# Two tables of a convolution stage: twelve taps of one half tile to the array's 32x32 parts, and another place for three merges

## The chip, the core and the metric

The kernel runs on one NeuronCore of a Trainium2 chip. Its engines work side by side, each through its own queue in order: TensorE (PE) multiplies matrices, VectorE (DVE) and ScalarE (ACT) do elementwise work, GpSimd (POOL) and SyncE (SP) mostly issue transfers. The metric is the device time of one execution in microseconds. Three runs of the kernel before took 1189.69, 1190.68 and 1196.95 us; the median is 1190.68 us.

## What is computed

A two-layer decoder trunk over 512 positions and 1024 channels. Layer 0 mixes with a state-space group and an attention; layer 1 mixes with the convolution module below. Each layer ends with two normalised residual steps. The change lies in the convolution of layer 1 and in what follows at once.

```python
def conformer_conv(x, w_pw1, b_pw1, w_dw, b_dw, ln_g, ln_b, w_pw2, b_pw2):
    h = x @ w_pw1 + b_pw1
    val, gate = jnp.split(h, 2, axis=-1)
    h = val * jax.nn.sigmoid(gate)
    h = lax.conv_general_dilated(            # causal, depthwise, 31 taps
        h, w_dw[:, None, :], window_strides=(1,), padding=[(CONV_SIZE - 1, 0)], ...)  + b_dw
    h = jax.nn.silu(layer_norm(h, ln_g, ln_b))
    return h @ w_pw2 + b_pw2
...
x = layer_norm(DEEPNORM_ALPHA * x + mix, ln1_g[layer], ln1_b[layer])
```

## The kernel before

Channels lie on partitions. The 1024 channels are eight tiles of 128, numbered 0 to 7, and a tile holds all 512 positions, or, where work is split, two halves of 256 positions (`HALVES`). A product of float32 matrices is made of three products of parts (`gemm`, line 225): each weight and each activation is kept as a high and a low part, and high x high, low x high and high x low are summed in PSUM. So one projection tile is 24 matmuls.

The convolution stage is written as a list of tokens, `CONV_ORDER`, that `step` works off one by one. After each token `in_order` chains every PE, DVE and ACT instruction of it behind the one before on its engine, so the list is the order of these three queues. A token is a letter, a tile, and, where it has a third character, a half (`40` is tile 4, first half; `41` its second half):

- `g`: the projections of a tile, value (`pv`) and gate (`pg`), 24 matmuls each; then a sigmoid on ACT (`csg`) and a product on DVE that writes the tile `hp`. `u` is the value projection alone, so that a later `g` of the same half has only the gate left.
- `v`: one part of the taps of a tile on DVE (`taps_dve`): each tap is one SCALAR_TENSOR_TENSOR into `cy` or `cz` in turn. A full tile's taps come in 5 parts, a half tile's in 4 (`PARTS`). The first part also makes ACT open `cy` and `cz` with the two last taps. `f` is the same in one go, for tiles with few or no taps on DVE. At the end `cy` and `cz` are summed and the tile is added to the running sum `sc` of its half, from which the mean comes.
- `p`: the first `PE_TAPS[half][tile]` taps on PE (`taps_32`, line 1126): for each tap four matmuls on 32x32 parts of the array, one for each group of 32 channels, with diagonal weights `D` that DVE makes (`d`, line 1134). The taps land in four PSUM tiles `cw`, since tap t uses column group t mod 4.
- `c`: ACT copies the four `cw` to SBUF (`cq`, line 1140). `m`: four PE matmuls sum them into `cn` (`merge`, line 1146). ACT or DVE then puts `cn` into `cy`.
- `M`, `Q`, `n`: the layer norm over channels of one half. `M` makes the mean on PE (`mpc`), subtracts it on DVE, squares on ACT (`sqc`) and adds on DVE. `Q` makes the variance on PE (`vpc`) and its inverse root: a table load and one activation (`rc`) on ACT, three steps on DVE (`tc`, `rc`). Each `n` takes two tiles: DVE multiplies `cy` by `rc`, ACT applies silu (another table load ahead of the first), and the result is split into `csh` (ACT) and `csl` (DVE).
- `t`: one output tile of the next projection `tld` (24 matmuls of 256 positions on all eight `csh`/`csl`), added to X on DVE. From the first `t` on the list runs inside `tail_norm_lead`, which makes the remaining `t` of both halves and the next norm.
- `x`: scales X on ACT.

PSUM has six tiles `nps` for projections, `cw` and `tld`, and two `stp` for `cn`, `mpc` and `vpc`. `hid` tiles (16) hold `hp`, `cz`, `D` and `cq`.

```python
PE_TAPS = ((0, 0, 24, 0, 0, 24, 31, 31), (0, 0, 0, 0, 0, 0, 31, 31))
PARTS = (5, 4)
```

Only tile 4 and tile 7 have tokens by halves. So the second row of `PE_TAPS` matters for these two: before, tile 4's second half has all its 29 remaining taps on DVE, 7, 7, 7 and 8 in the four `v41`.

## Time and profile before

| | before |
|---|---|
| three runs | 1189.69, 1190.68, 1196.95 us |
| the profiled execution's own time | 1188.93 us |
| its span in the trace | 1187.2 us |
| PE busy | 98 % |
| DVE, ACT busy | 64 %, 43 % |
| TensorE's mean granted clock | 0.993 |
| convolution stage, from tile 2's projections to the first `tld` | about 651 to 762 us in the span |

A row of the timeline gives start, duration, engine, line, operation, output and inputs, shapes and, in brackets, how long the engine had been idle and what ended it. Matmuls overlap: what one costs in a row of its kind is the distance of two starts, not its duration. A float32 matmul stands as two records in the trace (`cw`, `cn`, `mpc`, `vpc`), one of the split parts as one.

### The profile page before, as it was taken

The page shows a single profiled execution, that of the slowest core. Times are in us where ns is not written, and L with a number is a line of the kernel's source. Part 1 is how long each engine was busy: PE and PEld are TensorE (multiplying, and loading weights), DVE is VectorE, ACT ScalarE, POOL GpSimd, SP SyncE. Part 2 cuts the span into 40 slices and gives each one's busy share as a digit, 9 for nine tenths or more (in the row PEclk, how much of TensorE's full clock was granted, in tenths as well). Part 3 has the DMA queues.
Part 4 walks back from the last instruction along what each step waited for, and adds up shares of the span by engine and source line. Part 5 has one row for each costly group of instructions (what it writes and reads, how often), then busy time and mean ns, then how long its engine had stood idle before and what let it go on. Part 6 is the DMA issues. An engine that isn't in the chain of part 4 may idle for free.

```text
span 1187.2 us, 17722 instructions
## 1 busy us (share of the span) xinstructions
PE 1158.6 (98%) x7148; PEld 969.0 (82%) x7148; DVE 754.7 (64%) x1342; ACT 506.7 (43%) x798; POOL 67.0 (6%) x125
## 2 busy tenths in 40 slices
PE   9989999999999999999999999899999999999997
PEld 7777767799888888888999676699988888888885
DVE  7999876498545545546466899876833443434446
ACT  7857869336335335325223312552741421413220
POOL 1022211000000000000021120001000000000000
PEclk9999999999999999999999999899999999999999
DMA  9611321332788788779274451206241232323211
GB/s 213 168 50 51 93 67 57 105 107 80 244 286 293 238 287 297 247 274 306 91 263 161 145 181 35 73 3 211 89 143 61 99 124 71 107 86 110 73 51 71
DMA packets 132546, 169.58 MB, mean 143 GB/s; under 512 B 13874, under 2 KB 105778, under 8 KB 132464
## 3 DMA queue, kind: packets, MB, share of 16 engines
q1 hardware_dynamic: 123664, 136.96, 35.6%
q0 software_dynamic: 8640, 31.46, 7.9%
q8 instruction: 56, 0.92, 0.3%
q14 instruction: 26, 0.21, 0.1%
q10 hardware_dynamic: 160, 0.03, 0.0%
HBM read 132.12 MB, written 35.65 MB: 141 GB/s over the span
## 4 chain that ended last, share of the span: by engine, by line
PE 82%; DVE 8%; ACT 4%; DMA 3%; issue 1%; SPq 1%; POOL 0%; DVEq 0%; ACTq 0%; POOLq 0%
PE f L225 23%; PE g L1311 12%; PE acf L225 11%; PE tld L225 4%; PE tlb L225 4%; PE fl L225 3%; PE pv L225 3%; PE h L1295 3%; PE pg L225 3%; PE cw L1126 2%; PE tla L225 2%; PE acmo L225 2%; PE pl L225 2%; DVE wlo L102 1%; DMA raw<-in_ffn_w_dram 1%
## 5 line engine op out<-in xcount | busy, mean ns | idle before, releaser
L102 DVE TENSOR_TENSOR wlo<-raw,whi 128x1024 fp32r<-128x1024 f32 x176 | 213.3, 1223 | 199.7 <-ACT whi L101 197.5
L101 ACT CAST whi<-raw 128x1024 fp32r<-128x1024 f32 x176 | 182.1, 1049 | 322.0 <-PE g L1311 106.8
L1311 PE MATMUL g<-whi,hh 128*128 128x512 f32 x208 | 81.6, 392 | 0.0
L1311 PE MATMUL g<-whi,hl 128*128 128x512 f32 x208 | 81.6, 392 | 0.0
L1311 PE MATMUL g<-wlo,hh 128*128 128x512 f32 x208 | 81.5, 392 | 0.0
L225 PE MATMUL f<-xah,whi 128*128 128x512 f32 x208 | 81.0, 390 | 0.0
L225 PE MATMUL f<-xdh,whi 128*128 128x512 f32 x208 | 81.0, 389 | 0.0
L225 PE MATMUL f<-xdh,wlo 128*128 128x512 f32 x208 | 80.9, 389 | 0.0
L225 PE MATMUL f<-xal,whi 128*128 128x512 f32 x208 | 80.9, 389 | 0.0
L225 PE MATMUL f<-xdl,whi 128*128 128x512 f32 x208 | 80.9, 389 | 0.0
L225 PE MATMUL f<-xah,wlo 128*128 128x512 f32 x208 | 80.9, 389 | 0.0
L225 PE MATMUL acf<-hl,whi 128*128 128x512 f32 x192 | 75.6, 394 | 0.0
L225 PE MATMUL acf<-hh,whi 128*128 128x512 f32 x192 | 75.6, 394 | 0.0
L225 PE MATMUL acf<-hh,wlo 128*128 128x512 f32 x192 | 75.4, 393 | 0.0
L215 ACT CAST hh<-fr 128x512 fp32r<-128x512 f32 x64 | 39.7, 620 | 59.0 <-DVE fr L353 59.0
L216 DVE TENSOR_TENSOR hl<-fr,hh 128x512 fp32r<-128x512 f32 x64 | 44.1, 690 | 31.1 <-ACT hh L215 31.1
L353 DVE TENSOR_TENSOR fr<-fr 128x512 f32<-128x512 f32 x64 | 43.7, 685 | 14.4 <-ACT fr L154 14.4
L357 DVE SCALAR_TENSOR_TENSOR cy<-hp,wdw,cy 128x512 f32<-128x512 f32 (+1 forms) x81 | 52.2, 646 | 0.0
L357 DVE SCALAR_TENSOR_TENSOR cz<-hp,wdw,cz 128x512 f32<-128x512 f32 (+1 forms) x74 | 47.6, 643 | 0.0
L88 POOL DMA_DIRECT2D whi<-kepth x30 | 16.1, 536 | 556.8 <-PE tlb L225 386.3
L1311 PEld LDWEIGHTS g<-wlo,hh 128*128 128x128 f32 x208 | 39.1, 188 | 8.7
L1311 PEld LDWEIGHTS g<-whi,hl 128*128 128x128 f32 x208 | 39.0, 188 | 8.8
(631 smaller groups left out, 2890.4 us busy)
## 6 DMA issues: line engine op xcount, KB each, us to landing
raw<-in_ffn_w_dram SPq DMA_DIRECT2D x48, 1024.0 KB, 5.6
raw<-in_ffn_w_dram SPq DMA_DIRECT2D x32, 512.0 KB, 3.7
kepth<-whi SPq DMA_DIRECT2D x30, 512.0 KB, 3.6
keptl<-wlo SPq DMA_DIRECT2D x30, 512.0 KB, 9.3
whi<-kepth POOLq DMA_DIRECT2D x30, 512.0 KB, 3.6
wlo<-keptl POOLq DMA_DIRECT2D x30, 512.0 KB, 4.9
raw<-in_conv_w_pw_dram SPq DMA_DIRECT2D x12, 1024.0 KB, 7.1
raw<-in_mix_w_in_dram SPq DMA_DIRECT2D x16, 512.0 KB, 4.1
```

Source lines behind the costliest of these rows:

```text
L88: nc.gpsimd.dma_start(x, d)
L101: i0 = nc.scalar.copy(hi, raw).ins
L102: i1 = nc.vector.tensor_sub(lo, raw, hi.bitcast(F32)).ins
L215: i0 = S.copy(hi, src).ins
L216: i1 = V.tensor_sub(lo, src, hi.bitcast(F32)).ins
L225: ins = PE.matmul(ps[:, c0:c1], u[:, k, ksl], v[:, c0:c1], start=start and k == 0 and i == 0, stop=stop and k == n - 1 and i == 2).ins
L353: V.tensor_tensor(o, x, y, op=op)
L357: V.scalar_tensor_tensor(o, x, s, y, op0=op0, op1=op1)
L1126: PE.matmul(cps[j, c0][g][C, :], Ds[j][t // 16][R, t % 16, :], hps[j][R, t + c0 : t + c1], start=t < 4, stop=t >= n - 4, tile_position=(R. ...
L1295: PE.matmul(ps, u, v, start=k == 0 and i == 0, stop=k == nk - 1 and i == 2)
L1311: PE.matmul(pss[b], u, v[:, kk, :], start=k + kk == 0 and i == 0, stop=k + kk == nb - 1 and i == 2)
```

## The change

Two tables are rewritten, and nothing else.

```diff
-PE_TAPS = ((0, 0, 24, 0, 0, 24, 31, 31), (0, 0, 0, 0, 0, 0, 31, 31))
+PE_TAPS = ((0, 0, 24, 0, 0, 24, 31, 31), (0, 0, 0, 0, 12, 0, 31, 31))
-CONV_ORDER = "d2 g0 g1 v0 v0 g2 v0 v0 g3 p2 v1 c2 x0 v1 v1 v1 m2 f2 v0 g4 v1 v3 v3 g5 d5 v3 g6 p5 d7 d6 v3 c5 v3 m5 f5 g70 p6 v40 v40 c6 v40 m6 f6 v40 p70 c70 u71 m70 f70 M0 g71 v41 Q0 v41 p71 n0 n0 n0 n0 v41 t c71 v41 t m71 f71 t t M1 t Q1 n1 n1 n1 n1".split()
+CONV_ORDER = "d2 g0 g1 v0 v0 g2 v1 v0 v0 g3 p2 v1 c2 x0 v1 v1 v0 g4 m2 f2 v1 v3 v3 g5 d5 v3 g6 p5 d7 d6 v3 c5 v3 g70 m5 f5 p6 v40 d4 v40 c6 v40 u71 m6 f6 v40 p70 c70 v41 m70 f70 p41 M0 g71 v41 Q0 c41 p71 m41 n0 n0 n0 n0 v41 t c71 v41 t m71 f71 t M1 Q1 n1 n1 n1 n1".split()
```

Tile 4's second half now has 12 taps on PE (`p41`: 48 matmuls, with `d4`, `c41` and `m41`) and 17 on DVE, 4, 4, 4 and 5 in the four `v41`. The merges `m2`, `m5`, `m6` stand behind `g4`, `g70` and `u71`. One part `v1` stands ahead of `g3`. The first `v41` stands ahead of `m70`; none stands between `Q0` and `n0` any more, where `c41`, `p71` and `m41` stand. Of the `t`, three instead of four stand ahead of `M1`, and none between `M1` and `Q1`; the others follow.

On PE, the first merge (`cw2`, `cn2` are tile 2's taps and their merge, `pv4`, `pg4` tile 4's projections, `pv5` tile 5's). Before:

```order
L1126 MATMUL cw203_6330<-hp2_6177,D21_6148 32x512
L1146 MATMUL cn20_6470<-cq200_6436,mask_3281 32x512
...
L1146 MATMUL cn20_6470<-cq203_6439,mask_3281 32x512
L225 MATMUL pv40_6506<-xbh0_5585,whi130_6186 128x512
```

In the change:

```order
L1126 MATMUL cw203_6339<-hp2_6177,D21_6148 32x512
L225 MATMUL pv40_6486<-xbh0_5585,whi130_6186 128x512
...
L225 MATMUL pg40_6487<-xbh7_5599,wlo131_6191 128x512
L1146 MATMUL cn20_6540<-cq200_6442,mask_3281 32x512
...
L1146 MATMUL cn20_6540<-cq203_6445,mask_3281 32x512
L225 MATMUL pv50_6593<-xbh0_5585,whi132_6194 128x512
```

The 48 matmuls of tile 4's projection now stand between the taps and their merge. `m5` and `m6` moved in the same way, behind 48 and 24 matmuls.

On ACT, from the gate of tile 7's second half (`csg7256`) to the first silu. Before:

```order
L160 ACTIVATE csg7256_7332<-pg7256_7245,PV_86 128x256
L154 ACTIVATE cy4_7056<-hp4_6497,PV_86,wdw_3280 128x256
L154 ACTIVATE cz4_7057<-hp4_6497,wdw_3280 128x256
L156 ACT_TABLE_LOAD
L160 ACTIVATE rc0_7349<-vpc0_7344,cb_83 128x256
L156 ACT_TABLE_LOAD
L160 ACTIVATE cy0_6162<-cy0_6162,PV_86 128x256
```

In the change:

```order
L160 ACTIVATE csg7256_7392<-pg7256_7092,PV_86 128x256
L156 ACT_TABLE_LOAD
L160 ACTIVATE rc0_7404<-vpc0_7399,cb_83 128x256
L1140 COPY cq42560_7427<-cw42560_7286 128x256
L1140 COPY cq42561_7428<-cw42561_7287 128x256
...
L1140 COPY cq42563_7430<-cw42563_7289 128x256
L156 ACT_TABLE_LOAD
L160 ACTIVATE cy0_6162<-cy0_6162,PV_86 128x256
```

The two openings of tile 4's second half went ahead of the mean, and the four copies of its taps came in between `rc` and the second table load.

On DVE, from the inverse root to the first normalised tile. Before:

```order
L357 SCALAR_TENSOR_TENSOR tc0_7350<-vpc0_7344,rc0_7349 128x256
L353 TENSOR_TENSOR tc0_7350<-tc0_7350,rc0_7349 128x256
L357 SCALAR_TENSOR_TENSOR rc0_7349<-tc0_7350,rc0_7349 128x256
L357 SCALAR_TENSOR_TENSOR cz4_7057<-hp4_6497,wdw_3280,cz4_7057 128x256
...
L353 TENSOR_TENSOR cy0_6162<-cy0_6162,rc0_7349 128x256
L353 TENSOR_TENSOR cy1_6427<-cy1_6427,rc0_7349 128x256
```

In the change:

```order
L357 SCALAR_TENSOR_TENSOR tc0_7405<-vpc0_7399,rc0_7404 128x256
L353 TENSOR_TENSOR tc0_7405<-tc0_7405,rc0_7404 128x256
L357 SCALAR_TENSOR_TENSOR rc0_7404<-tc0_7405,rc0_7404 128x256
L353 TENSOR_TENSOR cy0_6162<-cy0_6162,rc0_7404 128x256
L353 TENSOR_TENSOR cy1_6252<-cy1_6252,rc0_7404 128x256
```

The seven taps that stood between `rc` and the first normalised tile are gone from there.

## Rows read from the trace of the kernel before

**Rows 1.** The page, section 1 (busy time, share of the span, instructions of each engine) and the line of section 2 with the granted TensorE clock in 40 slices of the span.

```profile
PE 1158.6 (98%) x7148; PEld 969.0 (82%) x7148; DVE 754.7 (64%) x1342; ACT 506.7 (43%) x798; POOL 67.0 (6%) x125
PEclk9999999999999999999999999899999999999999
```

**Rows 2.** Busy time of each engine in stretches of the span: from and to, length, PE, PE weight loads, DVE, ACT, POOL with their instructions in brackets, granted clock, DMA share, GB/s.

```profile
720.00:740.00 20.00, 19.38 (x419) 13.01 (x430) 19.76 (x42) 4.62 (x9) 0.00 (x0) 1.00 0.01 3
740.00:760.00 20.00, 17.17 (x452) 13.15 (x448) 16.79 (x45) 8.95 (x19) 2.11 (x4) 1.00 0.32 109
775.00:800.00 25.00, 25.00 (x196) 24.39 (x197) 17.80 (x50) 15.17 (x29) 0.12 (x1) 1.00 0.00 1
800.00:1150.00 350.00, 349.92 (x1760) 297.56 (x1759) 167.07 (x240) 122.21 (x174) 6.21 (x12) 1.00 0.32 104
```

**Rows 3.** Timeline of PE: the merges of tiles 2, 5 and 6, and that of tile 7's first half (128x256).

```profile
675.27 2.51 PE L1146 MATMUL cn<-cq,mask 128*32 128x512 f32 x8 [0.69 <-ACT cq L1140]
...
717.78 2.51 PE L1146 MATMUL cn<-cq,mask 128*32 128x512 f32 x8 [0.62 <-ACT cq L1140]
...
735.41 2.51 PE L1146 MATMUL cn<-cq,mask 128*32 128x512 f32 x8 [0.62 <-ACT cq L1140]
...
746.38 0.64 PE L1146 MATMUL cn<-cq,mask 128*32 128x256 f32 x8
```

**Rows 4.** Timeline of PE, 737 to 762 us without the projections: taps of tile 7's first half, mean, variance, taps of its second half, first matmul of `tld`.

```profile
737.86 4.60 PE L1126 MATMUL cw<-hp,D 32*32 32x256 f32 x218
...
742.66 0.72 PE L1126 MATMUL cw<-hp,D 32*32 32x256 f32 x30 [0.21 <-issue]
...
748.24 0.67 PE L915 MATMUL mpc<-sc,ones 128*128 128x256 f32 x2 [1.22 <-DVE sc L353]
...
752.08 1.99 PE L915 MATMUL vpc<-sqc,ones 128*128 128x256 f32 x8 [0.30 <-DVE sqc L353]
754.00 3.39 PE L1126 MATMUL cw<-hp,D 32*32 32x256 f32 x160
758.48 2.06 PE L1126 MATMUL cw<-hp,D 32*32 32x256 f32 x88 [1.09 <-issue]
761.87 0.39 PE L225 MATMUL tld<-csh,whi 128*128 128x256 f32 x1 [1.33 <-ACT csh L215]
```

**Rows 5.** Timeline of PE: the first matmul of the second `tld` tile, the merge behind it, the first matmul of the third tile, and the mean of the second half, which stands 48 matmuls later.

```profile
769.52 0.41 PE L225 MATMUL tld<-csh,whi 128*128 128x256 f32 x1
...
774.27 0.64 PE L1146 MATMUL cn<-cq,mask 128*32 128x256 f32 x8
774.84 0.38 PE L225 MATMUL tld<-csh,whi 128*128 128x256 f32 x1
...
780.69 0.59 PE L915 MATMUL mpc<-sc,ones 128*128 128x256 f32 x2
```

**Rows 6.** Busy time in stretches of 4 us, columns as in rows 2; the number behind the five engines is the granted clock (1.00 is 2.4 GHz, 0.50 is 1.2 GHz).

```profile
760.00:764.00 4.00, 2.52 (x28) 1.44 (x13) 2.87 (x9) 3.12 (x7) 0.00 (x0) 0.92 0.00 0
764.00:768.00 4.00, 4.00 (x15) 3.14 (x14) 3.20 (x9) 3.85 (x9) 0.00 (x0) 0.50 0.00 0
...
772.00:776.00 4.00, 4.00 (x31) 3.46 (x30) 3.93 (x11) 0.48 (x1) 0.00 (x0) 0.80 0.00 0
```

**Rows 7.** Timeline of DVE: product of tile 3 and the two full-width taps behind it, diagonals of tile 5 (768 columns in two), then from the sum of tile 4's first half to the last low part of the first half.

```profile
668.55 0.75 DVE L357 SCALAR_TENSOR_TENSOR hp<-pv,PV,csg 128x512 f32<-128x512 f32 x1 [2.14 <-ACT csg L160]
669.25 0.75 DVE L357 SCALAR_TENSOR_TENSOR cy<-hp,wdw,cy 128x512 f32<-128x512 f32 x1
669.92 0.75 DVE L357 SCALAR_TENSOR_TENSOR cz<-hp,wdw,cz 128x512 f32<-128x512 f32 x1
...
708.96 1.01 DVE L1134 TENSOR_TENSOR D<-mask,wdw 128x512 f32<-128x512 f32 x2
...
745.10 0.43 DVE L353 TENSOR_TENSOR sc<-sc,cy 128x256 f32<-128x256 f32 x1
747.67 0.42 DVE L353 TENSOR_TENSOR sc<-sc,cy 128x256 f32<-128x256 f32 x1 [2.14 <-ACT cy L154]
...
752.96 0.48 DVE L357 SCALAR_TENSOR_TENSOR hp<-pv,PV,csg 128x256 f32<-128x256 f32 x1
...
756.23 0.42 DVE L357 SCALAR_TENSOR_TENSOR tc<-vpc,rc 128x256 f32<-128x256 f32 x1
...
757.56 0.48 DVE L357 SCALAR_TENSOR_TENSOR cz<-hp,wdw,cz 128x256 f32<-128x256 f32 x1
...
760.33 0.75 DVE L353 TENSOR_TENSOR cy<-cy,rc 128x256 f32<-128x256 f32 x2
...
768.45 0.43 DVE L216 TENSOR_TENSOR csl<-cy,csh 128x256 fp32r<-128x256 f32 x1 [0.52 <-ACT csh L215]
```

**Rows 8.** Timeline of ACT: the copies of tile 7's first half, then from the first opening of tile 4's second half to the first silu.

```profile
743.55 1.20 ACT L1140 COPY cq<-cw 128x256 f32<-128x256 f32 x4 [4.89 <-PE cw L1126]
...
752.83 0.59 ACT L154 ACTIVATE cy<-hp,PV,wdw 128x256 f32<-128x256 f32 x1
...
753.83 1.28 ACT L156 ACT_TABLE_LOAD   x1
755.12 0.48 ACT L160 ACTIVATE rc<-vpc,cb 128x256 f32<-128x256 f32 x1
...
760.78 0.60 ACT L160 ACTIVATE cy<-cy,PV 128x256 f32<-128x256 f32 x1 [3.88 <-DVE cy L353]
```

## The prediction

> **What bounds the kernel now.** I read the page first: PE is busy 98% of the span and its clock is full in all slices but one, the slice near 770 us [rows 1]. Then the stretches: from 775 to 1150 us PE has no idle time to speak of (25.00 of 25, 349.92 of 350) [rows 2]. So whatever brings PE through the convolution stage earlier arrives whole at the end, and the question is what PE waits for there. In that stage DVE is as full as PE (19.76 and 19.38 of 20 us from 720 to 740), and from 740 to 760 us neither is (17.17 and 16.79) [rows 2]: there they wait for each other. Third, the timeline. PE loses 0.69, 0.62 and 0.62 us ahead of the three full-width merges, which then run at the pace of ACT's copies, 2.51 us each, while the half-width merge with its copies long done takes 0.64 [rows 3]. PE then waits 1.22 us for the mean's sum, 0.30 for the squares, and 1.33 for the first normalised tile [rows 4]. DVE has two gaps: 2.14 us until tile 3's gate is through ACT, and 2.14 us until tile 7's merged taps are [rows 7]. Last, the clock: PE is busy 2.52 us of 4 from 760 to 764, the granted clock is 0.50 (1.2 GHz) in the next stretch, and it comes back at about 773.6 (0.80 in 772 to 776) [rows 6]. The second `tld` tile runs in that fall: 24 matmuls from 769.52 to 774.27, 4.75 us; behind it 48 of them take 780.69 - 774.84 = 5.85, that is 2.93 for 24 [rows 5].

> **The change step by step**, in the time of the profiled execution (1188.93 us; its span is 1187.2).

> *Step 1, the mean of the first half.* Before, it waited for PE, then ACT, then DVE: merge until 747.02 [rows 3], `cy` on ACT, DVE's `sc` at 747.67 [rows 7], `mpc` at 748.24 [rows 4]. On DVE everything else for it was done at 745.10 + 0.43 = 745.53. Now both sides move.
> DVE: the `v1` ahead of `g3` has five taps, at 669.92 - 669.25 = 0.67 us [rows 7] 3.4 us, which fills the 2.14 us gap; the rest displaces work that had to come anyway: -2.14. The diagonals `d4` have 384 columns; 768 cost 1.01 us [rows 7]: +0.5. The first `v41` ahead of `f70` has four half-width taps. Seven take 760.33 - 757.56 = 2.77 us [rows 7], so 0.396 each: +1.6. The sum `sc` of tile 7 can start at 745.53 - 2.14 + 0.5 + 1.6 = 745.5 instead of 747.67: 2.2 us earlier, and DVE's second gap is gone.
> PE: is it ready by then? The three merges move behind projections that have no need of the copies. Without the wait a full-width merge costs at least 0.64 (the half-width row) and at most the 2.51 of now; I take twice the half-width row, 1.28, since it streams twice the columns. Saved: 3 x 2.51 + 0.69 + 0.62 + 0.62 - 3 x 1.28 = 5.6 us. Against it, `u71` no longer covers tile 7's copies (1.20 us [rows 8]): `m70` now waits about 0.6 and runs at the copies' pace, some 1.3 us more. `m70` ends at 747.02 - 5.6 + 1.3 = 742.7. Then `p41`: 48 of the taps' matmuls are 96 records, and 248 take 743.38 - 737.86 = 5.5 us [rows 4], so 2.1 us: done at 744.8, 1.2 us ahead of the mean at 748.24 - 2.2 = 746.0. So the cost of the added taps on PE lies in a wait that is there anyway; without that cover it would be 2.1 us. The projection `u71` is only moved. The six PSUM tiles hold `u71`'s two and four of `cw70`, then of `cw41`, which waits for the copies that `m70` waits for anyway: nothing more.

> *Step 2, from the mean to the first silu.* Before: 748.24 to 760.78 on ACT. The two openings between `csg` and the table load (752.83 to 753.83 [rows 8]) go ahead of the mean, so the load ends 1.0 us earlier, at 754.1 in the old count, and the variance ends at 752.08 + 1.99 = 754.07 [rows 4]: `rc` starts 1.0 earlier. On DVE only four taps stand behind `hp` (752.96 + 0.49 + 1.6 = 755.05), so `tc` starts at 755.05 instead of 756.23, its three steps take 757.56 - 756.23 = 1.33 as before, and the seven taps behind them (2.77) are gone: the first normalised product starts at 756.4 instead of 760.33. ACT is later than that: behind `rc` (until 754.6) come four copies, 1.2 us, and the second table load, 1.28 us [rows 8]: silu at 757.1 instead of 760.78, 3.7 us earlier. Without the copies the DVE side would set it at 756.8; they cost 0.3. With step 1 the first half is normalised 5.9 us earlier, its last low part at 768.45 - 5.9 = 762.6.

> *Step 3, PE up to `tld`.* `p71` needs PSUM tiles that `c41`'s first copies free: the variance ends 754.07 - 2.2 = 751.9, but `rc` ends at 752.4 and two copies are done at 753.0. So a new wait of 1.1 us. With the 6.5 us of before (754.00 to 760.54, the pause of 1.09 in it) `p71` ends at 759.5, the added merge `m41` at 760.2, and the first `tld` tile's 24 matmuls could end at 763.2. The last low part ends at 763.0, with two matmuls behind it: 763.3. PE and the norm meet, so neither the 1.1 us nor `m41` shows; without that balance they would cost up to 1.7. I take 763.4 for the second tile's start, 6.1 earlier than 769.52.

> *Step 4, the clock.* Before, PE trickled through the first `tld` tile, at the pace of silu and split, before and in the fall. Now that tile finds about five of its eight inputs ready. I take it that the fall goes: the second tile takes 2.93 instead of 4.75, 1.8 us less. If it stays, see the first rival.
> [...]

> *Step 5, the second half.* Twelve taps less on DVE are 4.75 us, the added sum with `cn` +0.4. DVE has 9 taps left behind the first half's split, 3.6 us, and is ready for the second mean at about 768; PE comes to it after `m71` and one more `t` at 763.4 + 2.9 + 0.6 + 2.9 = 769.8. No wait before (the mean stands in the row without one [rows 5]), none now. The `t` behind `M1` cover the rest, as 62 of them did.

> Sum: 6.1 + 1.8 = 7.9 us. 1188.93 - 7.9 = 1181.0. The profiled execution lies 1.75 under the median of the three runs (1190.68); with half of that I say **1182.0 us**.

> **Rivals.** *The clock falls again in this stage.* For it: the wait at the mean, then taps on 32x32 parts. Against it: before there were waits of 1.22 and 0.30 at 748 to 752 with no fall. A fall like the one here lasts some 10.2 us (0.64 of the stretch to 764, the two after it, 1.6 of that to 776 [rows 6]); at 24 matmuls in 4.75 instead of 2.93 it loses 10.2 x (1 - 2.93/4.75) = 3.9 us: **1185.9**.
> *PE is late for the mean.* The merges gain nothing by the move: 2.51 us is what they cost at full width, and the switch between projection and merge costs what the wait did. Then `p41` ends at 744.8 + 5.6 = 750.4, 4.4 us behind DVE: **1186.4**. Against it: the half-width row of 0.64.
> *The change is worth only its second part:* the DVE gap at tile 3 is not filled because ACT's openings of tile 1 come late. Then DVE sets the mean at 747.6: 2.1 less, **1184.1**.
> *Slower.* The clock falls while PE waits at the mean, at 745, and does not return while the sparse work lasts. Then the work up to the second `tld` tile (gate 3.2 us, variance 2.0, `p71` 5.5, `m41` 0.6, 48 matmuls 5.9: 17.2) takes between 1.62 (4.75/2.93) and 2 times as long; I take 1.8. That is 13.8 us, of which 1.1 is hidden in the wait for `c41`: 12.7 later, **1194.7**. It decides when falls cost more than the 7.9 gained, at 7.9/(1 - 1/1.8) = 18 us of half clock. Against it: the one fall here lasted 10.2 us, and the same sparse work before, 737 to 762 us, ran at full clock up to 763 [rows 6].

> **The numbers.** My forecast, 1180 to 1184.5, has 0.62; the second clock fall 0.15; PE late 0.08; the second part alone 0.08; slower by the lasting fall 0.04; better than 1178.8 (step 1 or 2 worth more than summed) 0.03. From 1178.5 to 1187.5 holds the first four and part of the last, over 0.8. A measurement of this kernel tells about 1% from no change, 11.9 us: faster than 1178.8 has 0.03 (the last case), slower than 1202.6 has 0.02 (half of the lasting fall), the rest, 0.95, is within 1%.

> **What would show it.** In the changed kernel: merges of tiles 2, 5, 6 without idle time and near 1.3 us; no gap on DVE ahead of tile 3's `hp` or ahead of tile 7's sum; PE idle 1 to 2 us ahead of the first `mpc`, then ahead of `p71`'s third group; silu 8.5 to 9 us behind that `mpc` (12.5 now); the first `tld` tile in about 3 us and a full clock throughout; the mean of the second half 9 to 11 us earlier on the span's scale, but the end of the span about 8. I am wrong if PE, not DVE, comes last at the mean, or if the clock's row shows a half anywhere in 740 to 780 us.

## The result, and the profile after

The changed kernel takes 1183.66 us (median of 7 runs, 1181.19 to 1186.86), the kernel before in the same job 1192.13 us (7 runs, 1189.69 to 1196.95): ratio 0.993, 95% interval 0.991 to 0.9949. The forecast was 1182.0, 1.66 less. The profiled execution took 1183.44 us, its span is 1181.7 us.

The two profiled executions do not enter the convolution stage at the same time: tile 2's product on DVE, with which it begins, starts at 657.67 before and at 658.95 after. I count from that product below. To the end of the span it is then 529.53 us before and 522.75 after, 6.78 less; a second profile of the changed kernel gave 521.74.

The three merges (timeline of PE, compare [rows 3]):

```profile
688.21 1.06 PE L1146 MATMUL cn<-cq,mask 128*32 128x512 f32 x8
...
723.64 1.06 PE L1146 MATMUL cn<-cq,mask 128*32 128x512 f32 x8
...
736.25 1.07 PE L1146 MATMUL cn<-cq,mask 128*32 128x512 f32 x8
```

No idle time stands ahead of them, and each takes 1.06 instead of 2.51. Then PE up to the third `tld` tile, without projections (compare [rows 4, 5]); 766.13 begins the second `tld` tile, 769.66 the third:

```profile
737.25 4.02 PE L1126 MATMUL cw<-hp,D 32*32 32x256 f32 x193
743.44 1.41 PE L1126 MATMUL cw<-hp,D 32*32 32x256 f32 x55 [2.17 <-issue]
745.32 1.45 PE L1146 MATMUL cn<-cq,mask 128*32 128x256 f32 x8 [0.47 <-ACT cq L1140]
746.70 2.13 PE L1126 MATMUL cw<-hp,D 32*32 32x256 f32 x96
748.75 0.70 PE L915 MATMUL mpc<-sc,ones 128*128 128x256 f32 x2
...
752.61 1.99 PE L915 MATMUL vpc<-sqc,ones 128*128 128x256 f32 x8 [0.30 <-DVE sqc L353]
754.54 0.62 PE L1126 MATMUL cw<-hp,D 32*32 32x256 f32 x4
755.57 4.21 PE L1126 MATMUL cw<-hp,D 32*32 32x256 f32 x185 [0.41 <-ACT cq L1140]
760.19 1.45 PE L1126 MATMUL cw<-hp,D 32*32 32x256 f32 x59 [0.42 <-issue]
761.57 0.64 PE L1146 MATMUL cn<-cq,mask 128*32 128x256 f32 x8
762.14 0.38 PE L225 MATMUL tld<-csh,whi 128*128 128x256 f32 x1
...
766.13 0.28 PE L225 MATMUL tld<-csh,whi 128*128 128x256 f32 x1
...
769.10 0.64 PE L1146 MATMUL cn<-cq,mask 128*32 128x256 f32 x8
769.66 0.38 PE L225 MATMUL tld<-csh,whi 128*128 128x256 f32 x1
```

The mean at 748.75 has no bracket: PE came last there. Three rows above it stands the larger part of why: in the middle of `p70`, behind 193 of its 248 rows (a row is one record of a matmul), PE stood 2.17 us for nothing that the profile shows ("issue"); before it was 0.21 [rows 4]. DVE's timeline (compare [rows 7]): tile 3's product, the sum ahead of the first `v41`, its first tap, and the sum behind it.

```profile
670.96 0.71 DVE L357 SCALAR_TENSOR_TENSOR hp<-pv,PV,csg 128x512 f32<-128x512 f32 x1
...
745.44 0.43 DVE L353 TENSOR_TENSOR sc<-sc,cy 128x256 f32<-128x256 f32 x1
746.62 0.48 DVE L357 SCALAR_TENSOR_TENSOR cy<-hp,wdw,cy 128x256 f32<-128x256 f32 x1 [0.76 <-ACT cy L154]
...
748.21 0.42 DVE L353 TENSOR_TENSOR sc<-sc,cy 128x256 f32<-128x256 f32 x1
```

ACT's timeline (compare [rows 8]): copies of `p70`, the first opening of tile 4's second half, then from the inverse root to the first silu.

```profile
744.89 1.20 ACT L1140 COPY cq<-cw 128x256 f32<-128x256 f32 x4 [6.75 <-PE cw L1126]
745.96 0.63 ACT L154 ACTIVATE cy<-hp,PV,wdw 128x256 f32<-128x256 f32 x1
...
754.77 0.47 ACT L160 ACTIVATE rc<-vpc,cb 128x256 f32<-128x256 f32 x1
755.15 1.19 ACT L1140 COPY cq<-cw 128x256 f32<-128x256 f32 x4
756.35 1.28 ACT L156 ACT_TABLE_LOAD   x1
757.65 0.60 ACT L160 ACTIVATE cy<-cy,PV 128x256 f32<-128x256 f32 x1
```

Both gaps of DVE in [rows 7] are filled (no bracket at 670.96 and 748.21), but a new one of 0.76 shows how PE's pause reaches DVE: the copies of `p70` wait for it, the openings stand behind the copies on ACT, and the first `v41` waits for the openings. From the mean to the first silu it is now 757.65 - 748.75 = 8.90 instead of 12.54. The clock (stretches as in [rows 6]) stays full where it was half:

```profile
764.00:768.00 4.00, 3.85 (x27) 3.22 (x26) 3.30 (x10) 2.34 (x7) 0.00 (x0) 1.00 0.00 0
768.00:772.00 4.00, 4.00 (x37) 3.46 (x37) 3.86 (x11) 0.47 (x1) 0.00 (x0) 1.00 0.02 4
```

What came ahead of the pause: the load of the weights that follow, issued on POOL at 736.50, 0.18 us after the end of `u71` (now ahead of `p70`), which gave its slot free; it stood at 746.63 before. POOL's timeline:

```profile
736.50 0.53 POOL L88 DMA_DIRECT2D whi<-kepth  x1 [24.11 <-PE pv L225]
```

The DMA queues from 738 to 741 us (packets, MB, share of 16 engines); q0 carries that load, and no instructions came in this stretch:

```profile
q0 software_dynamic: 274, 1.00, 94.9%
```

The same from 741 to 742 us; q8 is read as TensorE's instructions (the section on the pause shows why), and one of its packets is called a fetch below:

```profile
q8 instruction: 1, 0.02, 6.1%
q0 software_dynamic: 2, 0.00, 0.3%
```

The load fills 94.9% of the DMA engines from 738 to 741; the one fetch starts at 741.08, and PE goes on 2.36 us later, at 743.44.

### The profile page after: what moved, and what is told of

It reads as the page before. It is cut to its first block, busy times and chain, and to the rows that moved or that the text cites. A ratio compares the mean times of both kernels' runs of the same rounds, so it can differ in the third digit from the quotient of the medians.

```text
span 1181.7 us, 17927 instructions
## 1 busy us (share of the span) xinstructions
PE 1154.5 (98%) x7252; PEld 966.1 (82%) x7252; DVE 752.0 (64%) x1332; ACT 507.9 (43%) x802; POOL 66.5 (6%) x125
## 4 chain that ended last, share of the span: by engine, by line
PE 83%; ACT 2%; DVE 1%; DMA 1%; issue 1%; POOL 0%; SPq 0%; DVEq 0%; ACTq 0%
PE f L225 24%; PE g L1311 12%; PE acf L225 11%; PE fl L225 5%; PE tlb L225 4%; PE tld L225 4%; PE pv L225 3%; PE h L1295 3%; PE pg L225 3%; PE cw L1126 3%; PE tla L225 2%; PE pl L225 2%; PE acmo L225 1%; PE gg L225 1%; PE gv L225 1%
## 5 line engine op out<-in xcount | busy, mean ns | idle before, releaser
L357 DVE SCALAR_TENSOR_TENSOR cy<-hp,wdw,cy 128x512 f32<-128x512 f32 (+1 forms) x75 | 49.3, 657 | 0.8 <-ACT cy L154 0.8
L1311 PEld LDWEIGHTS g<-whi,hh 128*128 128x128 f32 x208 | 39.1, 188 | 8.8
```

What stands on the lines that cost most here:

```text
L357: V.scalar_tensor_tensor(o, x, s, y, op0=op0, op1=op1)
L1311: PE.matmul(pss[b], u, v[:, kk, :], start=k + kk == 0 and i == 0, stop=k + kk == nb - 1 and i == 2)
```

## The experiments

One table for all, in us. The pause is that in `p70`. Mean is the start of the first `mpc`, merge that of the merge of tile 7's second half (769.10 above), end the end of the span, all counted from tile 2's product; in between stands the time from the mean to the first silu. "Half clock" lists the stretches of 4 us from 740 to 780 whose granted clock is under 0.9 (full is 1.00, the lowest here 0.50; in the 0.50 of before, matmuls of 256 columns start 0.213 us apart from 769.52 to 773.14, 1.2 columns a ns). A ratio is to the kernel before in the same job (medians 1192.13, 1193.79 for e1 to e4, 1190.91 for k1 to k4, 1191.88 for the last two). The profile of k4 is of the longest of its seven executions, 1189.25.

| kernel | time | ratio, interval | pause | mean | to silu | merge | end | half clock |
|---|---|---|---|---|---|---|---|---|
| before | 1192.13 | | 0.21 | 90.57 | 12.54 | 116.60 | 529.53 | 764 to 776 |
| the change | 1183.66 | 0.993, 0.991-0.9949 | 2.17 | 89.80 | 8.90 | 110.15 | 522.75 | none |
| k1 merges only | 1188.74 | 0.9983, 0.9964-1.0002 | 2.20 | 89.27 | 13.65 | 115.47 | 528.55 | 744 to 752, 764 to 772 |
| k2 change without taps on PE | 1187.53 | 0.9973, 0.9959-0.9988 | 2.13 | 89.46 | 11.79 | 112.69 | 526.46 | 748 to 756 |
| k3 taps only | 1188.08 | 0.9979, 0.9963-0.9994 | 0.30 | 92.38 | 10.79 | 114.62 | 527.63 | none |
| k4 first `v41` only | 1186.10 | 0.9956, 0.994-0.9973 | 0.27 | 91.34 | 9.80 | 113.95 | 526.54 | 768 to 776 |
| e1 `u71` back | 1184.68, one run | | 0.33 | 88.81 | 8.90 | 109.16 | 521.73 | none |
| e2 `u71` held | 1182.53, one run | | 0.83 | 88.29 | 8.90 | 108.63 | 521.39 | none |
| e3 opening early | 1187.78, one run | | 1.87 | 90.37 | 8.91 | 110.72 | 523.37 | 748 to 752 |
| e4 both | 1183.49 | 0.9915, 0.9889-0.9942 | none | 88.57 | 8.90 | 108.91 | 521.55 | none |
| the change again | 1183.72 | 0.9927, 0.9904-0.995 | 1.58 | 89.14 | 8.90 | 109.49 | 521.74 | none |
| e2 again | 1181.77 | 0.9905, 0.9887-0.9923 | 0.28 | 88.05 | 8.90 | 108.38 | 521.00 | none |

### Where the late mean came from

Theory: `u71`'s earlier place brings its weight load forward, that load delays the instructions of `p70`, and the pause makes the mean late. Instead of it, DVE's new wait for ACT's openings could be the cause. e1 puts `u71` back behind `c70`; e2 leaves it ahead of `m6`, but holds its last three matmuls back behind `p70`, so that its weights come free late; e3 puts the first `v41`, and with it the openings, ahead of the copies; e4 joins e2 and e3.

```diff
 e1
-... v40 c6 v40 u71 m6 f6 v40 p70 c70 v41 ...
+... v40 c6 v40 m6 f6 v40 p70 c70 u71 v41 ...
 e2 (w71: the matmuls of u71 on the last k)
-... u71 m6 f6 v40 p70 c70 v41 ...
+... u71 m6 f6 v40 p70 w71 c70 v41 ...
-    def gemm(ps, w, ksl, xs, c0, c1, start=True, stop=True):
+    def gemm(ps, w, ksl, xs, c0, c1, start=True, stop=True, k0=0):
...
-        for k in range(n):
+        for k in range(k0, n):
...
-                gemm(vps, ws[j][0], slice(0, P), xs, c0, c1)
+                gemm(vps, ws[j][0], slice(0, P), xs[: KT - 1] if only_value else xs, c0, c1, stop=not only_value)
...
+        elif k == "w":
+            gemm(ps[j][0], ws[j][0], slice(0, P), xs, c0, c1, start=False, k0=KT - 1)
 e3
-... p70 c70 v41 ...
+... p70 v41 c70 ...
```

> The changed kernel with the value projection u71 behind c70 again, as it stood before the change, and m6 therefore directly behind c6. Places are told from the start of tile 2's hp on DVE (658.95 in the changed kernel). Theory: the 2.17 us pause in tile 7's first-half taps comes from the 1 MB weight load that the end of u71 releases, and that the next 16 KB block of PE instructions queues behind. With u71 later the load starts after the taps, so the pause there is at most 0.5 us; m6 waits 0.6 again and runs 2.5 instead of 1.07 (2.0 lost), m70 is covered again (0.8 won). First mean 0 to 1 us earlier than in the changed kernel. Rival: taps at half width use up instructions faster than they come, load or not; the pause of 1 to 2.2 us stays, and the first mean is 1 to 2 us later.

> The changed kernel with one edit: the last 3 of u71's 24 matmuls stand behind p70, so that its weight buffers, and with them the load of 1 MB, come free only then. PE does the same work. Theory (the load delays the instruction block): pause in tile 7's first-half taps at most 0.5 us instead of 2.17; p41 ends about 1.7 us earlier; then DVE is last at the mean, and the mean comes 0.7 to 0.9 us earlier against tile 2's hp. Rival (rate of instructions alone): pause within 0.4 us of 2.17, mean unchanged.

> The changed kernel with the first v41 ahead of c70 instead of behind it, so that ACT opens tile 4's second half ahead of the copies and DVE need not wait 0.76 us for it. In the changed kernel PE's p41 and DVE's sum end together at the first mean (748.75). Theory (PE, paused, is last as well): the mean stays within 0.2 us. Rival (DVE behind ACT's openings alone is last): the mean comes 0.7 us earlier.

> Both edits of the two runs before: u71's last 3 matmuls behind p70 and the first v41 ahead of c70. Theory: neither PE (no pause) nor ACT's openings hold the first mean; DVE's own taps do, and the mean comes 0.8 to 1.4 us earlier than in the changed kernel; time 1 to 1.5 us below it, ratio to the kernel before 0.991 to 0.993. Rival: no better than the changed kernel, 0.993 or above, the pause still there.

With the load late the pause is short or gone (0.33, none, and 0.83 in e2, more than the 0.5 expected) and the mean 1.0 to 1.5 us earlier than in the change's first profile, 0.3 to 0.9 earlier than in its second, whose pause was 1.58. In e1 the third merge waits and runs as before (0.62, 2.51), and still its mean is the earlier one.

With the opening early alone (e3) the pause stays (1.87), and the mean, expected within 0.2 us, is 0.57 later (90.37). PE alone sets it there: DVE's sum ends at 751.24, and the mean starts at 753.00 (PE and DVE of e3):

```profile
746.49 1.41 PE L1126 MATMUL cw<-hp,D 32*32 32x256 f32 x55 [1.87 <-issue]
...
750.81 0.43 DVE L353 TENSOR_TENSOR sc<-sc,cy 128x256 f32<-128x256 f32 x1
...
753.00 0.70 PE L915 MATMUL mpc<-sc,ones 128*128 128x256 f32 x2
```

A stretch of half clock that the change did not have makes the work between the pause and the mean 1.20 longer (6.51 against 5.31); its single time says no more. So the pause keeps the mean late, and the place of the openings does not mend it. e4, timed, is at 0.9915, no different from the change by the intervals.

One thing varies that no edit here made: tile 2's taps at the start of the stage. They took 8.17 and 8.07 us in the change's profiles, 8.07 in e1, 7.52 and 6.92 in the two of e2, 7.80 in e4 and 6.86 before, though PE's order up to them is the same. That does not explain the earlier mean: e1 has the long ones, and in e2 and e4 PE is idle ahead of the mean for longer (0.71, 1.64, 1.49) than the long ones would cost it (0.65, 1.25, 0.37).

e2 was then run again beside the change:

> The changed kernel with the last three matmuls of u71 held back behind p70, so that its weights come free, and are reloaded, 6 us later. Theory (the fetch, not PE's work, made the mean late): 1.1 to 1.5 us faster than the changed kernel beside it. Rival (what is won at the mean is lost before the end of the stage): the same as the changed kernel within 0.4 us.

> The changed kernel once more, on one chip with the next. Theory and rival alike: 0.993 of before.

PE in e2's second profile:

```profile
736.11 4.06 PE L1126 MATMUL cw<-hp,D 32*32 32x256 f32 x196
740.45 1.39 PE L1126 MATMUL cw<-hp,D 32*32 32x256 f32 x52 [0.28 <-issue]
742.31 1.44 PE L1146 MATMUL cn<-cq,mask 128*32 128x256 f32 x8
743.68 2.13 PE L1126 MATMUL cw<-hp,D 32*32 32x256 f32 x96
747.45 0.70 PE L915 MATMUL mpc<-sc,ones 128*128 128x256 f32 x2 [1.64 <-DVE sc L353]
```

PE is now done 1.64 us ahead of the mean and DVE comes last, as the forecast had it for the change itself. e2 is 1.95 us faster in the medians; its six runs (1180.03 to 1182.15) lie under five of the change's six (1181.70 to 1187.05), though the two intervals overlap and 1.1 to 1.5 were expected. In the profiles the mean is 1.09 earlier, the merge 1.11 and the end 0.74, so from the mean to the merge nothing is lost.

### What the pause is

In the change's trace the pauses in `p70` and `p71` fall at the records 9409 and 10177 of PE and its weight loads, counted from the start: 768 apart, three times 256. A third, of 0.65 us in tile 2's taps, falls at 7617, seven times 256 ahead of the first. If a block of 256 begins at every such record, there are 57 beginnings in the change and 56 before, and q8 has as many packets in either trace: so q8 is read as TensorE's instructions. s16 and s48 repeat tile 2's first tap on 32 columns 16 and 48 times ahead of its real taps, which write over it: 64 and 192 records more. The edit of s16 (s48 has 12 for the 4):

```diff
+        for t in range(4 if j == 2 else 0):
+            for g in range(4):
+                R, C = part_of(0, g)
+                PE.matmul(cps[j, c0][g][C, :32], Ds[j][0][R, 0, :], hps[j][R, c0 : c0 + 32], start=True, stop=True, tile_position=(R.start, C.start))
```

> The changed kernel with 16 extra matmuls of 32 columns ahead of tile 2's taps; they are 64 records of matmul and weight load, and write what the first tap then overwrites. Theory (the pause in p70 is the wait for a block of 256 instructions, whose fetch comes when the block before it begins and stands behind the packets of u71's early weight load): the pause falls 64 records, 32 rows of cw, earlier: behind row 161 of p70's 248 instead of 193, and is longer by what the taps gain on the fetch, 2.2 to 2.9 us; the pause in p71 falls behind row 153 instead of 185. Rival (the pause belongs to a place in the program, such as the second half of the diagonals or a semaphore): behind row 193 as before, 2.17 us.

> The same with 48 extra matmuls, 192 records. Theory: the blocks of p70 begin ahead of its row 1 and behind its rows 97 and 225; the fetch for row 97 starts ahead of the weight load's packets and is in time, the one for row 225 starts when they end: no pause behind row 193, none at 97, one of 0.8 to 1.6 us behind row 225. Rival (a place in the program): behind row 193, 2.17 us.

`p70` and `p71` in s16, then in s48:

```profile
740.18 3.39 PE L1130 MATMUL cw<-hp,D 32*32 32x256 f32 x161
745.34 2.05 PE L1130 MATMUL cw<-hp,D 32*32 32x256 f32 x87 [1.77 <-issue]
...
758.11 3.58 PE L1130 MATMUL cw<-hp,D 32*32 32x256 f32 x153 [0.41 <-ACT cq L1144]
762.31 2.08 PE L1130 MATMUL cw<-hp,D 32*32 32x256 f32 x91 [0.62 <-issue]
```

```profile
737.87 4.65 PE L1130 MATMUL cw<-hp,D 32*32 32x256 f32 x225
743.97 0.69 PE L1130 MATMUL cw<-hp,D 32*32 32x256 f32 x23 [1.45 <-issue]
...
756.72 4.84 PE L1130 MATMUL cw<-hp,D 32*32 32x256 f32 x217 [0.41 <-ACT cq L1144]
762.22 0.71 PE L1130 MATMUL cw<-hp,D 32*32 32x256 f32 x27 [0.66 <-issue]
```

The pause moved to the row that was named, 161 and 225, in `p71` too (153 as named; 217 follows by the same count). So it belongs to the count of instructions and not to a place in the program. e2 agrees: its pause stands behind row 196, three later, since it holds back three matmuls with their weight loads. (The single times, 1186.11 and 1184.72, hold the extra matmuls and say nothing of the pause.) Its size in s16 (1.77) is under the 2.2 to 2.9 expected: the fetch there started at 742.88 while the load's packets ran until 745.12, so they did not bar it.

In s48 the next block, again 256 records on, begins at the mean, and PE stood there too:

```profile
750.01 0.59 PE L915 MATMUL mpc<-sc,ones 128*128 128x256 f32 x2 [1.28 <-issue]
```

Its fetch started at 747.67, 3.70 us after the block ahead of it began (743.97), though the load's packets had ended at 741.83. So these 1.28 us had no load beside them; what delayed this fetch stays open.

### The parts apart

k1 moves the three merges alone (with `u71`), k2 is the change without `d4 p41 c41 m41`, k3 is before with these alone, k4 is before with the first `v41` ahead of `m70` and none between `Q0` and `n0`.

```diff
 k1
-... m2 f2 v0 g4 ... m5 f5 g70 ... m6 f6 v40 p70 c70 u71 m70 ...
+... v0 g4 m2 f2 ... g70 m5 f5 ... u71 m6 f6 v40 p70 c70 m70 ...
 k2 (against the change; 0 for 12 in PE_TAPS)
-... v40 d4 v40 c6 ... f70 p41 M0 g71 v41 Q0 c41 p71 m41 n0 ...
+... v40 v40 c6 ... f70 M0 g71 v41 Q0 p71 n0 ...
 k3 (12 for 0 in PE_TAPS)
-... v40 v40 c6 ... f70 M0 g71 v41 Q0 v41 p71 n0 ...
+... v40 d4 v40 c6 ... f70 p41 M0 g71 v41 Q0 v41 c41 p71 m41 n0 ...
 k4
-... c70 u71 m70 f70 M0 g71 v41 Q0 v41 p71 n0 ...
+... c70 u71 v41 m70 f70 M0 g71 v41 Q0 p71 n0 ...
```

> The order of before, with only the three merges moved as in the change (m2 behind g4, m5 behind g70, m6 behind u71, which stands ahead of it); no taps of tile 4's second half on PE, no tap part moved on DVE. Theory (the merges' wait on ACT's copies was real, and once it is gone DVE and the late instruction block set the mean): the three merges run in 1.06 each without idle time, p70 shows a pause of about 2 us because u71 stands ahead of it, the mean comes 1 to 2 us earlier than before, everything behind it lasts as before (mean to first silu 12.5), the half clock near 765 us stays; 1 to 2 us faster than before in all. Rival (the merges carry most of the 7 us): mean 5 us earlier, 5 us faster or more.

> The changed kernel without the twelve taps on PE (d4, p41, c41 and m41 left out, tile 4's second half with all 29 taps on DVE); merges, u71, tap parts and t as in the change. Theory (order carries the gain, the taps little): PE is free 2.1 to 2.9 us earlier at the mean, DVE has three more half-width taps ahead of it (1.2 us, less 0.5 for the diagonals) and three more ahead of the inverse root: mean 0 to 0.5 us earlier than in the change, mean to first silu 9.5 to 10 instead of 8.9, no half clock near 765; 0 to 1.5 us slower than the change, so 6 to 7.5 us faster than before. Rival (the taps on PE are what fills PE and removes the half clock): the half clock is back near 765 us and the time is within 3 us of before.

> The order of before with the twelve taps alone (d4, p41, c41, m41 put in as in the change; merges, u71, tap parts and t where they were). Theory (the taps pay only where the merges have made PE early): PE comes to the mean 2.1 to 2.9 us later than before where 1.2 us of wait are there, so the mean is 0.9 to 1.7 us later; mean to first silu 1.8 us shorter, since three taps less stand on either side of the inverse root but the two openings still stand between gate and table load; the half clock stays: 0 to 1 us faster than before. Rival (the taps carry the gain): 4 us faster or more.

> The order of before with one edit: the first part of tile 4's second half stands ahead of m70, and none stands between Q0 and n0 (all 29 taps stay on DVE). Theory: DVE's gap of 2.14 us ahead of tile 7's sum takes 2.14 of the 2.8 us of seven taps, so the mean is 0.6 us later; the openings end ahead of the mean and seven taps less stand ahead of the first normalised product, so mean to first silu is 2.8 us shorter (9.7); 2.2 us faster than before if the half clock near 765 us stays, 4 us if it goes. Rival (DVE's taps only change places): mean later by what the silu gains, 0 us.

k1 came as the theory had it, 1.3 us at the mean and 0.2% in all (its interval reaches 1.0002), with one thing not expected: the clock fell a first time at the mean (0.62 and 0.53 from 744 to 752), and from there to silu it took 13.65 instead of the 12.5 expected. k4 too: mean 0.8 later, silu 2.74 closer, and part of the half clock gone (0.75 and 0.83 from 768 to 776, where before has 0.50 and 0.80). k2 was expected 6 to 7.5 us faster than before and gained 3.4. Here is why, in stretches of k2 and PE at its mean:

```profile
744.00:748.00 4.00, 1.45 (x8) 0.55 (x8) 3.43 (x10) 2.29 (x7) 0.00 (x0) 0.99 0.01 2
748.00:752.00 4.00, 3.10 (x12) 2.95 (x13) 2.62 (x9) 1.41 (x5) 0.00 (x0) 0.50 0.00 0
752.00:756.00 4.00, 4.00 (x22) 3.87 (x21) 2.60 (x8) 2.36 (x7) 0.53 (x1) 0.65 0.00 0
```

```profile
744.26 1.45 PE L1146 MATMUL cn<-cq,mask 128*32 128x256 f32 x8 [0.47 <-ACT cq L1140]
748.90 1.19 PE L915 MATMUL mpc<-sc,ones 128*128 128x256 f32 x2 [3.19 <-DVE sc L353]
754.91 1.46 PE L915 MATMUL vpc<-sqc,ones 128*128 128x256 f32 x6
```

Without `p41` PE waits 3.19 us at the mean, behind a pause of 2.13; it is busy 1.45 us of 4, and the granted clock is 0.50 next. From mean to variance it is 6.01 instead of the change's 3.86: 2.15 lost. The rival had the half clock come back, though near 765. In k3 the taps cost at the mean a little more than the theory said (1.8 later; 0.9 to 1.7 expected) and gave 1.75 on the way to silu, but no stretch is at half clock, so it gained 2.8 instead of 0 to 1: at the first silu it is 0.06 behind the kernel before, at the merge 1.98 ahead, and between the two lies the half clock of before. The clock of all timed executions says the same, 0.9954 in the mean of k3's twelve against 0.9916 in the 29 of before beside them. So the taps are worth more as filler for PE than as work taken from DVE: with them the clock is 1.00 in every stretch from 740 to 780 in k3 and in the change, without them it falls to 0.50 in before, k1 and k2 and to 0.75 in k4. They are no guarantee, since in e3 it fell once with them, to 0.57 in 748 to 752.

## Why the prediction was right, and where it was not

**Step 1 was mis-sized**: 2.2 us forecast, 0.77 measured (1.43 in the second profile). DVE's side held: where the pause is gone, DVE sets the mean 2.28 and 2.52 us earlier than before (e2), 2.00 in e4. What failed is PE's side, `p41` "done at 744.8, 1.2 us ahead of the mean". It ended at 746.70 + 2.13 = 748.83, which is 747.55 when the 1.28 between the two entries into the stage are taken off: 2.75 late. Of these, 2.1 are `p70`. I took 5.5 us for it from before and called `u71` "only moved"; its weight load moved with it, and `p70` took 743.44 + 1.41 - 737.25 = 7.60. Another 1.31 are tile 2's taps, 8.17 against 6.86, for which the sum had no term; 0.65 of that is a pause of the same kind, the rest no run explains. The merges gave 0.66 back, at 1.06 each instead of my 1.28. By these numbers (an estimate that no run tests) either loss alone would have left PE done at about the time at which DVE sets the mean; both together made it last.

So what the prediction named as its own sign of error, PE last at the mean, came true, though the time came out near. Rows of before had the pauses in small ("0.21 <-issue", "1.09 <-issue" [rows 4]); I read them as constants.

**Step 2 held**: 3.64 us shorter against 3.7, with the order that was worked out: `rc`, copies, table load, silu.

**Step 3** was off by step 1 alone: the second `tld` tile starts 4.67 us earlier, not 6.1. The wait for `c41` was 0.41, not 1.1, since two of `p71`'s four groups run ahead of it.

**Step 4 held**: the clock stays full and the second tile takes 769.10 - 766.13 = 2.97 instead of 4.75. k2 and k1 show that this was near: the rival of a second fall, and the first half of the slower rival (a fall while PE waits at the mean), are what happens there without the twelve taps. Such a fall lasted nearly 7 us (in k2 1 - clock is 0.01, 0.50 and 0.35 in three stretches of 4 us, 3.44 us in sum, and half clock counts half) and cost 1.11 us on the way to silu in k1 and 2.15 up to the variance in k2, not 12.7. That the fall would go was my estimate from the one fall of before (PE busy 2.52 us of 4, then 0.50); no run shows what ends a fall.

**Step 5 held**: the second mean stands at 772.64 without a wait.

The sum was 7.9. At the third `tld` tile 769.66 - 658.95 against 774.84 - 657.67 makes 6.46, at the end 6.78 and, in the second profile, 7.79; with the pause mended (e2, e4) it is 7.98 to 8.53. That PE's gain in this stage arrives at the end was right.

That the time came out within 1.66 us is in part luck. I put the base between a profile and a median of three, at 1189.9; it became 1192.13 over seven, 2.2 more. From median to median the gain was 8.47, more than the 7.9, while the first profile shows less, 6.78. The executions of one kernel lie 6 to 7 us apart, so the times cannot tell a gain of 6.8 from one of 8.5; the stages can, and there step 1 was short.

## What to carry to other kernels

A step that is moved takes along the loads that its end releases (here from 746.63 to 736.50): look up which weight slot it frees, and what runs while the new load's packets do. A small "issue" gap can be the place where that hurts: in taps of 0.0208 us a row the one of `p70` was 0.21 before and 2.17 with the load beside it. And extra work placed in an engine's wait can pay by the clock (0.9954 in k3, 0.9916 in before beside it), so try the parts of a change together as well as apart: k3 and k4 alone gave 0.2 and 0.4%, and k1 nothing that is clear of zero.

## What the hardware showed that was not expected

```profile
q8 instruction: 57, 0.93, 0.3%
```

That is 16 KB a packet. Taps of half width run at 4.02/193 = 0.0208 us a row, a row being one of a matmul's two records with its weight load, two instructions; so 256 instructions pass in 128 x 0.0208 = 2.7 us, while PE went on 2.36 us after the fetch began. In `p70` of seven profiles in which `u71`'s load runs beside it (the change twice, k1, k2, e3, s16, s48) the fetch starts 2.03 to 2.86 us after the block ahead of it began, and the pause is 1.45 to 2.20 us. In seven in which it does not (before, e1, e2 twice, e4, k3, k4) it starts 0.40 to 1.15 us after that, and the pause is 0 to 0.83.

TensorE's granted clock fell around the mean in k1 (0.62 and 0.53 from 744 to 752), k2 (0.50 and 0.65 from 748 to 756) and e3 (0.57 from 748 to 752), each behind a pause (2.20, 2.13, 1.87) and a wait of 0.47 for the copies close behind it, and not in the change with 2.17 and 0.47. What divides e3 from the change, which both have `p41`, no run here settles.
